# Value and query projections ahead of the key chain, and modulation sums tied in order, in a one-core transformer block

## The chip, the core and the metric

The kernel runs on one core of a Trainium2 chip. The time is that of the device from start to end of one execution, in microseconds (us). The engines are TensorE (PE, matrix products and transposes), VectorE (DVE), ScalarE (ACT), GpSimd (POOL) and SyncE (SP); here SP issues nearly all loads of weights, POOL most other transfers. Each engine runs its own list of instructions in order, and waits on semaphores for the others.

## What is computed

One layer of a diffusion transformer block for 256 latent and 256 context tokens of width 2048, in float32. In short:

```
mod = silu(c) @ w_ada + b_ada            # sh1, sc1, g1, sh2, sc2, g2
h = (x * (1 + sc1) + sh1) @ w_in         # all projections, context tokens for the states
branches = hyena(h), hgrn2(h), gated_deltanet(h)
y = sum(sigmoid(gate) * (branch @ w_branch)) @ w_out
x = layernorm(ALPHA * x + g1 * y) * ln1_g + ln1_b
x = layernorm(ALPHA * x + g2 * (relu(u @ w1) ** 2 @ w2)),  u = x * (1 + sc2) + sh2
```

The DeltaNet branch takes keys, values and queries through a convolution of three taps and a silu, and scales keys and queries to unit length in each head; it needs the products of keys with keys and of queries with keys in chunks of 64 (Gram blocks). The Hyena branch needs filters: a small network, a window and a transform (DFT) for each of 2 orders and 4 column blocks.

## The kernel before

**Weights.** A block of weights (128 x 1024 numbers, 512 KB) is loaded by SP into one of four slots with the tag `wraw` (L143), cast by ACT to a rounded high part `whi` (L138), and DVE takes the rest `wlo` (L139). PE then makes three products for each block (high x high, low x high, high x low; L218 to L220, L474, L476). There are four `whi` and three `wlo` slots. A slot is free again when its last reader is done; the loads wait for that on SP in their order.

**Order.** The program is written as one sequence, and a scheduler then decides the order on each engine, by its own model of durations; it may move an instruction ahead of others if the data allow it. `keep_in_program_order` ties an instruction behind the one of its engine that was written just before it. `beside(name, steps, rate)` puts a generator of small steps beside the stream of weights: each call of `wload` lets it advance by its rate.

**Modulation sums.** The columns of `w_ada` for g1, sh2, sc2 and g2 are not multiplied on PE: DVE sums them as `acc = acc + a * csil` (L531, the first by L529), for 8 parts of 16 units, 128 x 1024 each (`ada_parts`). A unit loads its tile `aw` into a `wraw` slot, one ahead. Parts 0 to 5 (96 units) run beside the projections from the start of `dn_early` on; parts 6 and 7 (32 units) are a part of `first_norm`, beside the feed-forward weights, and load into a ring of eight places, `awr`.

**DeltaNet.** `dn_early` takes the keys (`kch`, in PSUM tiles `psk`) through `conv_silu` (an ACT scaling, taps on DVE at L501 to L505 in the tile `cy`, silu on ACT), the gates (`dn_gates`), the unit lengths (`unit_rows`: transposes, squares and a root on ACT, a scaling on DVE at L570, transposes back) and the Grams; then the queries likewise; then four blocks of values, each followed by two filter steps.

**Filters.** A step of `filt` (`filters`) is: two loads on POOL, four products with the small network's output (L278), window (L279), skip (L283), sum and difference (L286, L287, `smdf`), a split into `shl` (ACT L138, DVE L139), 30 products with the transform (L234 to L236), copies out (L294).

**First layer norm.** The last block of `w_out` makes its two token tiles one after the other. For each: residual (L1396, L1400), statistics (`bn_stats` L1402, `bn_aggr` L1407), root on ACT and reciprocal (L1409, L1445), scaling of `xr` (L1450 on DVE, L1452 on ACT), transposes, modulation to `u2t` (L1460 on DVE, L1463 on ACT), split into `u` (L138, L139). The feed-forward products then begin.

Of the kernel before, what the change touches and what calls it, by code (L numbers as in the profile page):

```python
# [16 lines left out]
P = 128  # L17
# [63 lines left out]
def tile_block(ctx: ExitStack, tc: tile.TileContext, A: dict, out: bass.AP):  # L81
# [10 lines left out]
    def slot(shape, tag, name, dt=F32):  # L92
        uid[0] += 1
        return sbp.tile(shape, dt, name=f"{name}_{uid[0]}", tag=tag, bufs=NB[tag])
# [14 lines left out]
    def page(name, *shapes, dt=F32):  # L109

        return cut(slot([P, 2048], "k8", name, dt), shapes)
# [5 lines left out]
    def sc_ps():  # L117
        uid[0] += 1
        return psp.tile([P, 512], F32, name=f"ps_{uid[0]}", tag="ps", bufs=4)
# [50 lines left out]
    def transpose(dst_ps, src):  # L170
        nc.tensor.transpose(dst_ps, src, ident)
# [281 lines left out]
    def proj_cm(wap, col0, ah, al):  # L453

        ps = mm_ps()
        for kb in range(4):
            wh, wl = wload(wap, kb * 4, 4, col0, 256)
            for ch in range(2):
                for k in range(4):
                    kt = kb * 4 + k  # L460
                    cm_block(ps[:, ch * T:(ch + 1) * T], wh, wl, ch, k, ah[:, kt, :], al[:, kt, :],
                             kt == 0 and ch == 0, kt == KT - 1)
        return ps.rearrange("p (c t) -> p c t", c=2)
# [48 lines left out]

    acc_d = dram([8, P, W], "acc_d")

    def ada_parts(parts, ring=None):
        def load(b, kt):
            a = slot([P, W], "wraw", "aw") if ring is None else ring[:, (b * KT + kt) % 8]
            nc.sync.dma_start(out=a, in_=w_ada[kt * P:(kt + 1) * P, 2 * D + b * W:2 * D + (b + 1) * W])
            return a

        for b in parts:
            acc = slot([P, W], "k4", "acc")
            ahead = None
            for kt in range(KT):
                a = ahead if kt else load(b, kt)
                if kt < KT - 1:
                    ahead = load(b, kt + 1)
                if kt == 0:
                    ts_(out=acc, in0=a, scalar1=csil[:, 0, kt:kt + 1], scalar2=None, op0=MUL)  # L529
                else:  # L530
                    stt(out=acc, in0=a, scalar=csil[:, 0, kt:kt + 1], in1=acc, op0=MUL, op1=ADD)  # L531
                if kt == KT - 1:
                    dma(out=acc_d[b], in_=acc)
                yield

# [11 lines left out]
    def unit_rows(ch, tok, tiles, extra, nm):  # L549

        n = 4 * tiles
        ss = cst.tile([P, n], F32, name=f"ss_{nm}")
        for tl in range(tiles):
            pt = sc_ps()
            for j in range(4):
                transpose(pt[:, j * P:(j + 1) * P], ch[:, j, tl * P:(tl + 1) * P])
            copy(out=tok[:, tl, :], in_=pt)
            for j in range(4):
                junk = slot([P, P], "k1", "junk")
                act(out=junk, in_=tok[:, tl, j * P:(j + 1) * P], func=AF.Square,  # L560
                    accum_out=ss[:, 4 * tl + j:4 * tl + j + 1])
        act(out=ss, in_=ss, func=AF.Sqrt, bias=eps[:, 0:1])
        nc.vector.reciprocal(out=ss, in_=ss)
        if extra != 1.0:
            ts_(out=ss, in0=ss, scalar1=extra, scalar2=None, op0=MUL)
        for tl in range(tiles):
            pt = sc_ps()
            for j in range(4):
                t = tok[:, tl, j * P:(j + 1) * P]
                ts_(out=t, in0=t, scalar1=ss[:, 4 * tl + j:4 * tl + j + 1], scalar2=None, op0=MUL)  # L570
                transpose(pt[:, j * P:(j + 1) * P], t)
            copy(out=ch[:, :, tl * P:(tl + 1) * P], in_=pt.rearrange("p (j t) -> p j t", j=4))
# [84 lines left out]
    def dn_early():  # L657
        kch = page("kch", (4, 512))
        for r in range(4):
            conv_silu(psk[r], dck, r, True, kch[:, r, :])  # L660
        dn_gates()
        ktok = page("ktok", (4, 512))
        unit_rows(kch, ktok, 4, 1.0, "k")
        dma(out=kt_d.rearrange("t p c -> p t c"), in_=ktok)
        KKd, qch = page("kkq", (16, 64), (4, T))
        kxq, QKd = page("kxq", (24, 64), (8, 64))
        KX, QX = kxq[:, 0:16, :], kxq[:, 16:24, :]
        def grams(tl, rhs, diag, cross):
            ps = sc_ps()
            for j in range(4):  # L670
                sl = slice(tl * P, (tl + 1) * P)
                mm(ps[:, j * P:(j + 1) * P], kch[:, j, sl], rhs[:, j, sl], start=True, stop=True)
            pv = ps.rearrange("p (j f t) -> p j f t", j=4, f=2)
            for f in range(2):
                pr_ = slice(f * 64, (f + 1) * 64)
                copy(out=diag[pr_, tl * 4:(tl + 1) * 4, :], in_=pv[pr_, :, f, :])
                copy(out=cross[pr_, tl * 4:(tl + 1) * 4, :], in_=pv[pr_, :, 1 - f, :])

        for tl in range(4):
            grams(tl, kch, KKd, KX)  # L680
        for f in range(2):
            for rep in range(2):
                dma(out=dk[:, :, rep, f].rearrange("t q i j -> i (t q) j"), in_=KKd[f * 64:(f + 1) * 64])
        dma(out=kc_d, in_=kch)
        for blk in range(2):
            ps = proj_cm(w_in, C_DQ + blk * 256, uxh, uxl)
            for ch in range(2):
                r = 2 * blk + ch
                conv_silu(ps[:, ch, :], dcq, r, False, qch[:, r, :])
        unit_rows(qch, page("qtok", (2, 512), (2, 512))[0], 2, float(P) ** -0.5, "q")  # L690
        for tl in range(2):
            grams(tl, qch, QKd, QX)
        for f in range(2):
            for rep in range(2):
                dma(out=dq[:, :, rep, f].rearrange("t q i j -> i (t q) j"), in_=QKd[f * 64:(f + 1) * 64])
        dma(out=q_d, in_=qch)
        dma(out=kx_d, in_=kxq)

        for blk in range(4):
            pss = proj_cm_ctx(C_DV + blk * 256)  # L700
            for ch in range(2):
                r = 2 * blk + ch
                y = slot([P, 512], "k2", "vy")
                conv_silu(pss[ch], dcv, r, True, y)
                pt = sc_ps()
                for i in range(4):
                    transpose(pt[:, i * P:(i + 1) * P], y[:, i * P:(i + 1) * P])
                vt = slot([P, 4, P], "k2", "vt")
                copy(out=vt.rearrange("p a b -> p (a b)"), in_=pt)
                dma(out=v_d[:, :, r * P:(r + 1) * P].rearrange("t p c -> p t c"), in_=vt)  # L710
            next(filt)
            next(filt)

    def dn_systems():

# [76 lines left out]
            yield  # L792
        dma(out=dx[1], in_=M[64:P])

    beside("ada", ada_parts(range(6)), 1.0)
    dn_early()


# [762 lines left out]
```

## Time and profile before

| | before |
|---|---|
| median of 3 runs (range) | 2377.84 us (2377.05 to 2380.38) |
| profiled execution, its span | 2378.33 us, 2376.6 us |
| PE busy, mean granted clock | 96%, 0.982 |
| DVE, ACT, POOL busy | 69%, 45%, 8% |
| DMA queues, share of 16 engines | 69%, 215 GB/s |

The profile is one execution. PE is busy when a product is in its pipeline, which also counts products that run at half clock; so a stretch is read by both its idle time and its granted clock. A wait is put down to what ended it last.

### The profile page before, as it was taken

The page shows a single profiled execution, that of the slowest core. Times are in us where ns is not written, and L with a number is a line of the kernel's source. Part 1 is how long each engine was busy: PE and PEld are TensorE (multiplying, and loading weights), DVE is VectorE, ACT ScalarE, POOL GpSimd, SP SyncE. Part 2 cuts the span into 40 slices and gives each one's busy share as a digit, 9 for nine tenths or more (in the row PEclk, how much of TensorE's full clock was granted, in tenths as well). Part 3 has the DMA queues.
Part 4 walks back from the last instruction along what each step waited for, and adds up shares of the span by engine and source line. Part 5 has one row for each costly group of instructions (what it writes and reads, how often), then busy time and mean ns, then how long its engine had stood idle before and what let it go on. Part 6 is the DMA issues. An engine that isn't in the chain of part 4 may idle for free.

```text
span 2376.6 us, 32445 instructions
## 1 busy us (share of the span) xinstructions
PE 2280.7 (96%) x12353; PEld 1950.4 (82%) x12353; DVE 1649.0 (69%) x2183; ACT 1077.1 (45%) x1465; POOL 180.8 (8%) x297
## 2 busy tenths in 40 slices
PE   7999898999999999999999999996999999999998
PEld 4778688989989989777888878885888888888886
DVE  6777467877789898976566656658964655655667
ACT  6665444434433443534443444434544544543542
POOL 0000221000200000012030020000000000000000
PEclk9999999999999999999999999998999999999999
DMA  9958767778663333578786898677976666666664
GB/s 333 343 183 258 228 181 223 243 254 249 202 178 98 107 94 111 137 217 275 232 250 220 285 314 257 204 233 266 303 247 194 186 190 191 186 192 190 195 204 150
DMA packets 296072, 511.18 MB, mean 215 GB/s; under 512 B 17526, under 2 KB 155217, under 8 KB 293324
## 3 DMA queue, kind: packets, MB, share of 16 engines
q1 hardware_dynamic: 271488, 422.63, 56.2%
q0 software_dynamic: 21648, 82.01, 11.4%
q10 hardware_dynamic: 2780, 4.47, 0.6%
q8 instruction: 97, 1.59, 0.3%
q14 instruction: 59, 0.48, 0.1%
HBM read 474.59 MB, written 34.45 MB: 214 GB/s over the span
## 4 chain that ended last, share of the span: by engine, by line
PE 68%; DMA 7%; DVE 5%; issue 2%; ACT 1%; POOL 0%; DVEq 0%; SPq 0%; ACTq 0%; POOLq 0%
PE mm L474 10%; PE mm L490 8%; PE mm L491 8%; PE mm L489 8%; PE mm L476 5%; PE mm L220 3%; PE mm L218 3%; PE mm L219 3%; DMA aw<-in_w_ada_dram 3%; PE mm L815 3%; PE mm L816 3%; PE mm L814 3%; DVE wlo L139 2%; DMA wraw<-in_w_in_dram 2%; PE ps L1045 1%
## 5 line engine op out<-in xcount | busy, mean ns | idle before, releaser
L138 ACT CAST whi<-wraw 128x1024 fp32r<-128x1024 f32 x584 | 613.6, 1052 | 910.1 <-PE mm L491 253.9
L139 DVE TENSOR_TENSOR wlo<-wraw,whi 128x1024 fp32r<-128x1024 f32 x584 | 711.7, 1221 | 382.2 <-PE mm L490 148.1
L474 PE MATMUL mm<-u,whi 128*128 128x512 f32 x1024 | 361.8, 400 | 9.3 <-DVE u L139 7.6
L220 PE MATMUL mm<-uh,wlo 128*128 128x256 f32 (+1 forms) x1024 | 340.4, 336 | 3.4 <-DVE wlo L139 3.3
L218 PE MATMUL mm<-uh,whi 128*128 128x256 f32 (+1 forms) x960 | 317.9, 331 | 12.8 <-DVE cy L505 12.8
L219 PE MATMUL mm<-ul,whi 128*128 128x256 f32 (+1 forms) x960 | 318.4, 332 | 0.0
L476 PE MATMUL mm<-u,wlo 128*128 128x256 f32 x1024 | 283.9, 282 | 1.2 <-DVE wlo L139 1.1
L474 PEld LDWEIGHTS mm<-u,whi 128*128 128x128 f32 x1024 | 191.9, 189 | 55.2 <-DVE u L139 7.8
L220 PEld LDWEIGHTS mm<-uh,wlo 128*128 128x128 f32 x1024 | 198.4, 194 | 22.8 <-DVE wlo L139 4.2
L218 PEld LDWEIGHTS mm<-uh,whi 128*128 128x128 f32 x960 | 186.4, 194 | 29.8 <-issue 9.2
L219 PEld LDWEIGHTS mm<-ul,whi 128*128 128x128 f32 x960 | 186.2, 194 | 15.4 <-issue 0.7
L476 PEld LDWEIGHTS mm<-u,wlo 128*128 128x128 f32 x1024 | 194.7, 190 | 4.2 <-DVE wlo L139 1.9
L491 PE MATMUL mm<-whi,h 128*128 128x512 f32 x480 | 187.2, 390 | 0.0
L490 PE MATMUL mm<-wlo,h 128*128 128x512 f32 x480 | 186.9, 389 | 0.2 <-DVE wlo L139 0.2
L489 PE MATMUL mm<-whi,h 128*128 128x512 f32 x480 | 185.7, 391 | 0.0
L531 DVE SCALAR_TENSOR_TENSOR acc<-aw,csil,acc 128x1024 f32<-128x1024 f32 x90 | 115.2, 1280 | 95.4 <-DMA aw<-in_w_ada_dram 95.3
L815 PE MATMUL mm<-wlo,uh 128*128 128x512 f32 x384 | 153.1, 399 | 2.9 <-DVE wlo L139 2.9
L814 PE MATMUL mm<-whi,uh 128*128 128x512 f32 x384 | 150.2, 400 | 3.0 <-ACT fk L960 1.6
L816 PE MATMUL mm<-whi,ul 128*128 128x512 f32 x384 | 151.5, 395 | 0.0
L490 PEld LDWEIGHTS mm<-wlo,h 128*128 128x128 f32 x480 | 90.1, 188 | 19.6 <-DVE wlo L139 0.6
L489 PEld LDWEIGHTS mm<-whi,h 128*128 128x128 f32 x480 | 90.1, 188 | 19.4 <-issue 0.7
L491 PEld LDWEIGHTS mm<-whi,h 128*128 128x128 f32 x480 | 90.1, 188 | 18.9 <-issue 0.2
(517 smaller groups left out, 3992.2 us busy)
## 6 DMA issues: line engine op xcount, KB each, us to landing
wraw<-in_w_in_dram SPq DMA_DIRECT2D x264, 512.0 KB, 4.6
wraw<-in_w_ff_dram SPq DMA_DIRECT2D x256, 512.0 KB, 4.3
aw<-in_w_ada_dram SPq DMA_DIRECT2D x96, 512.0 KB, 4.6
raw<-in_w_ada_dram SPq DMA_DIRECT2D x32, 1024.0 KB, 5.7
wraw<-in_w_branch_dram SPq DMA_DIRECT2D x48, 512.0 KB, 5.0
wraw<-in_w_out_dram SPq DMA_DIRECT2D x32, 512.0 KB, 4.6
awr<-in_w_ada_dram SPq DMA_DIRECT2D x32, 512.0 KB, 8.5
g_d<-gate POOLq DMA_DIRECT2D x24, 256.0 KB, 5.0
```

What stands on the lines that cost most here:

```text
L138: copy(out=hi, in_=src)
L139: tt_(out=lo, in0=src, in1=hi.bitcast(F32), op=SUB)
L218: mm(ps, wh[:, k, cs], ah, start=first, stop=False, skip_group_check=True)
L219: mm(ps, wh[:, k, cs], al, start=False, stop=False, skip_group_check=True)
L220: mm(ps, wl[:, k, cs], ah, start=False, stop=last, skip_group_check=True)
L474: mm(pss[ch], wh[:, k, cs], a[:, kt].rearrange("p s t -> p (s t)"), start=(kt == 0), stop=False, skip_group_check=True)
L476: mm(pss[ch][:, 0:T], wl[:, k, cs], a[:, kt, 0], start=False, stop=(kt == KT - 1), skip_group_check=True)
L489: mm(pss[i], a, wh[:, k, :], start=(kt == 0), stop=False)
L490: mm(pss[i], a, wl[:, k, :], start=False, stop=False)
L491: mm(pss[i], b, wh[:, k, :], start=False, stop=(kt == nk - 1))
L815: mm(pg[i], a, wl[:, k, :], start=False, stop=False)
L816: mm(pg[i], c, wh[:, k, :], start=False, stop=(kt == KT - 1))
```

## The change

Three things change. `ada_parts` ties each sum to the DVE instruction written before it, for all 8 parts. The first 24 of the 96 units of parts 0 to 5 load into a ring of four places, `aring`, two units ahead; the other 72 use `wraw` slots as before, one ahead; the units of parts 6 and 7 load up to six ahead into their ring. In `dn_early`, values and queries are written in blocks between the steps of the key chain, and the filter steps between these.

```diff
     acc_d = dram([8, P, W], "acc_d")
 
-    def ada_parts(parts, ring=None):
...
+    in_turn = tc.keep_in_program_order
+
+    def ada_parts(parts, ring=None, places=8, first=None, pinned=False):
+
+        units = [(b, kt) for b in parts for kt in range(KT)]
+        first = len(units) if first is None else first
+        got = []
+
+        def load():
+            n = len(got)
+            b, kt = units[n]
+            a = ring[:, n % places] if n < first else slot([P, W], "wraw", "aw")
+            ld = nc.sync.dma_start(out=a, in_=w_ada[kt * P:(kt + 1) * P, 2 * D + b * W:2 * D + (b + 1) * W])
+            if pinned:
+                in_turn(ld)
+            got.append(a)
+
+        acc = None
+        for n, (b, kt) in enumerate(units):
+            ahead = places - 2 if n + 1 < first and not pinned else 1
+            while len(got) <= n or (len(got) < len(units) and len(got) <= n + ahead
+                                    and (len(got) < first or len(got) <= n + 1)):
+                load()
+            a = got[n]
+            if kt == 0:
+                acc = slot([P, W], "k4", "acc")
+                in_turn(ts_(out=acc, in0=a, scalar1=csil[:, 0, kt:kt + 1], scalar2=None, op0=MUL))
+            else:
+                in_turn(stt(out=acc, in0=a, scalar=csil[:, 0, kt:kt + 1], in1=acc, op0=MUL, op1=ADD))
+            if kt == KT - 1:
+                dma(out=acc_d[b], in_=acc)
+            yield
...
-        dn_gates()
-        ktok = page("ktok", (4, 512))
-        unit_rows(kch, ktok, 4, 1.0, "k")
-        dma(out=kt_d.rearrange("t p c -> p t c"), in_=ktok)
-        KKd, qch = page("kkq", (16, 64), (4, T))
-        kxq, QKd = page("kxq", (24, 64), (8, 64))
-        KX, QX = kxq[:, 0:16, :], kxq[:, 16:24, :]
-        def grams(tl, rhs, diag, cross):
...
-        for tl in range(4):
-            grams(tl, kch, KKd, KX)
...
-        for blk in range(2):
-            ps = proj_cm(w_in, C_DQ + blk * 256, uxh, uxl)
-            for ch in range(2):
-                r = 2 * blk + ch
-                conv_silu(ps[:, ch, :], dcq, r, False, qch[:, r, :])
...
-        for blk in range(4):
+        def values(blk):
...
-            next(filt)
-            next(filt)
...
+        values(0)
+        next(filt)
+        dn_gates()
+        KKd, qch = page("kkq", (16, 64), (4, T))
+        queries(0)
+        ktok = page("ktok", (4, 512))
+        unit_rows(kch, ktok, 4, 1.0, "k")
+        dma(out=kt_d.rearrange("t p c -> p t c"), in_=ktok)
+        queries(1)
+        next(filt)
+        kxq, QKd = page("kxq", (24, 64), (8, 64))
+        KX, QX = kxq[:, 0:16, :], kxq[:, 16:24, :]
+        values(1)
+        for tl in range(4):
+            grams(tl, kch, KKd, KX)
+        for f in range(2):
+            for rep in range(2):
+                dma(out=dk[:, :, rep, f].rearrange("t q i j -> i (t q) j"), in_=KKd[f * 64:(f + 1) * 64])
+        dma(out=kc_d, in_=kch)
+        next(filt)
+        next(filt)
+        values(2)
+        unit_rows(qch, page("qtok", (2, 512), (2, 512))[0], 2, float(P) ** -0.5, "q")
+        next(filt)
+        next(filt)
+        values(3)
+        for tl in range(2):
+            grams(tl, qch, QKd, QX)
+        for f in range(2):
+            for rep in range(2):
+                dma(out=dq[:, :, rep, f].rearrange("t q i j -> i (t q) j"), in_=QKd[f * 64:(f + 1) * 64])
+        dma(out=q_d, in_=qch)
+        dma(out=kx_d, in_=kxq)
+        next(filt)
+        next(filt)
...
-    beside("ada", ada_parts(range(6)), 1.0)
+    beside("ada", ada_parts(range(6), slot([P, 4, W], "m16", "aring"), 4, 24), 1.0)
     dn_early()
```

In the first layer norm the order on DVE was as follows, for the second token tile (`awr` are the ring's tiles, `st` the statistics, `mv_a` mean and variance):

```order
L139 TENSOR_TENSOR u_2288_13722<-u2t_13867,u_2288_13722 128x4x128
L529 TENSOR_SCALAR acc_14763<-awr_14762,csil 128x1024
L1402 BN_STATS st_13180<-xr_13178 128x6
L531 SCALAR_TENSOR_TENSOR acc_14763<-awr_14762,csil,acc_14763 128x1024
L1407 BN_AGGR mv_a_13927<-st_13180 128x2
L531 SCALAR_TENSOR_TENSOR acc_14763<-awr_14762,csil,acc_14763 128x1024
L1409 RECIPROCAL mv_a_13927<-mv_a_13927 128x1
L531 SCALAR_TENSOR_TENSOR acc_14763<-awr_14762,csil,acc_14763 128x1024
L1445 SCALAR_TENSOR_TENSOR mv_a_13927<-mv_a_13927 128x1
L1450 TENSOR_SCALAR xr_13178<-xr_13178,mv_a_13927 128x512 x2
L531 SCALAR_TENSOR_TENSOR acc_14763<-awr_14762,csil,acc_14763 128x1024
L1460 TENSOR_SCALAR u2t_13938<-ps_13933,gm,bm 128x128
```

And with the change (lines of the changed kernel are some 26 higher there):

```order
L139 TENSOR_TENSOR u_2265_13699<-u2t_13844,u_2265_13699 128x4x128
L1428 BN_STATS st_13157<-xr_13155 128x6
L1433 BN_AGGR mv_a_13904<-st_13157 128x2
L1435 RECIPROCAL mv_a_13904<-mv_a_13904 128x1
L1471 SCALAR_TENSOR_TENSOR mv_a_13904<-mv_a_13904 128x1
L1476 TENSOR_SCALAR xr_13155<-xr_13155,mv_a_13904 128x512 x2
L1486 TENSOR_SCALAR u2t_13915<-ps_13910,gm,bm 128x128
L1486 TENSOR_SCALAR u2t_13928<-ps_13923,gm,bm 128x128
L1486 TENSOR_SCALAR u2t_13915<-ps_13910,gm,bm 128x128
```

The first twelve rows hold five sums of the ring's tiles around the statistics and the scaling; with the change they stand over 60 rows further on, among the feed-forward blocks.

On DVE, beside one of the last filter steps, before:

```order
L279 TENSOR_TENSOR win_2956<-ps_2964,win_2956 128x512
L139 TENSOR_TENSOR wlo_3700<-wraw_3697,whi_3699 128x1024
L284 MEMSET win_2956 1x256
L283 TENSOR_TENSOR win_2956<-win_2956,sk_2968 1x256
L286 TENSOR_TENSOR smdf_2972<-win_2956 128x512
L287 TENSOR_TENSOR smdf_2972<-win_2956 128x512
L139 TENSOR_TENSOR wlo_3738<-wraw_3735,whi_3737 128x1024
L139 TENSOR_TENSOR shl_2975<-smdf_2972,shl_2975 128x1024
L139 TENSOR_TENSOR wlo_3771<-wraw_3768,whi_3770 128x1024
```

With the change, one filter step of the same kind, in a stretch that has no weight split between `wlo_3155`, 57 rows up, and `wlo_3188` (`hyc` is the Hyena convolution, `aring` and `aw` are tiles of w_ada in the ring and in weight slots):

```order
L543 SCALAR_TENSOR_TENSOR acc_2348<-aring_1237,csil,acc_2348 128x1024
L284 MEMSET win_2871 1x256
L502 SCALAR_TENSOR_TENSOR hyc_3137<-mm_3010,colB,hyc_3137 128x4x63
L543 SCALAR_TENSOR_TENSOR acc_2348<-aw_2782,csil,acc_2348 128x1024
L286 TENSOR_TENSOR smdf_2887<-win_2871 128x512
L287 TENSOR_TENSOR smdf_2887<-win_2871 128x512
L543 SCALAR_TENSOR_TENSOR acc_2348<-aw_3041,csil,acc_2348 128x1024
L139 TENSOR_TENSOR shl_2890<-smdf_2887,shl_2890 128x1024
L543 SCALAR_TENSOR_TENSOR acc_2348<-aw_3104,csil,acc_2348 128x1024
L139 TENSOR_TENSOR wlo_3188<-wraw_3185,whi_3187 128x1024
L139 TENSOR_TENSOR wlo_3218<-wraw_3215,whi_3217 128x1024
```

Before, weight splits alternate with the filter's rows; now the sums stand among them and the weights behind. On SP, the loads that lead to `wraw_3185` were these before, for the weights `wraw_3097` to `wraw_3238` of the same projections:

```order
L143 DMA wraw_3097<-in_w_in_dram 128x4x256
L518 DMA aw_3127<-in_w_ada_dram 128x1024
L143 DMA wraw_3130<-in_w_in_dram 128x4x256
L143 DMA wraw_3175<-in_w_in_dram 128x4x256
L518 DMA aw_3205<-in_w_ada_dram 128x1024
L143 DMA wraw_3208<-in_w_in_dram 128x4x256
L143 DMA wraw_3238<-in_w_in_dram 128x4x256
```

And with the change:

```order
L143 DMA wraw_3011<-in_w_in_dram 128x4x256
L527 DMA aw_3041<-in_w_ada_dram 128x1024
L527 DMA aring_1237<-in_w_ada_dram 128x1024 x4
L143 DMA wraw_3044<-in_w_in_dram 128x4x256
L143 DMA wraw_3074<-in_w_in_dram 128x4x256
L527 DMA aw_3104<-in_w_ada_dram 128x1024
L143 DMA wraw_3107<-in_w_in_dram 128x4x256
L143 DMA wraw_3152<-in_w_in_dram 128x4x256
L527 DMA aw_3182<-in_w_ada_dram 128x1024
L527 DMA aring_1237<-in_w_ada_dram 128x1024 x4
L143 DMA wraw_3185<-in_w_in_dram 128x4x256
```

The tiles in weight slots come as often as before, one for one or two weights; the ring's loads stand between them, and the sums that free the slots are now in the order of the program.

## Rows read from the trace of the kernel before

**Rows 1.** Work of each engine, PE's granted clock and DMA share in two stretches.
```profile
165.00:425.00 260.00, 238.80 (x1467) 211.56 (x1466) 167.00 (x267) 123.70 (x221) 48.17 (x75) 0.95 0.72 222
...
1600.00:1652.70 52.70, 34.68 (x163) 29.08 (x162) 40.53 (x69) 21.62 (x37) 2.70 (x4) 0.81 0.75 262
```

**Rows 2.** Waits of PE in 165 to 425: engine, line, releaser, us, times, longest.
```profile
PE mm L218 <- DVE cy L505: 12.8, 4, 6.0
```

**Rows 3.** Waits of DVE in the same stretch.
```profile
DVE acc L531 <- DMA aw<-in_w_ada_dram: 31.2, 15, 5.3
```

**Rows 4.** DVE's timeline ahead of the key convolutions: start, us, instruction [idle before].
```profile
160.37 1.28 DVE L531 SCALAR_TENSOR_TENSOR acc<-aw,csil,acc 128x1024 f32<-128x1024 f32 x1 [2.33 <-DMA aw<-in_w_ada_dram]
```

**Rows 5.** PE's timeline in the first layer norm.
```profile
1634.43 3.45 PE L171 MATMUL ps<-idon,xr 128*128 128x128 f32 x16 [10.41 <-DVE xr L1450]
1645.49 0.79 PE L474 MATMUL mm<-u,whi 128*128 128x512 f32 x1 [7.61 <-DVE u L139]
```

**Rows 6.** DVE's timeline in the first layer norm, both token tiles.
```profile
1615.02 0.26 DVE L1407 BATCH_NORM_AGGREGATE mv_a<-st 128x2 f32<-128x24 f32 x1
...
1615.92 1.00 DVE L1450 TENSOR_SCALAR xr<-xr,mv_a 128x512 f32<-128x512 f32 x2
...
1623.52 0.69 DVE L139 TENSOR_TENSOR u<-u2t,u 128x512 fp32r<-128x512 f32 x1
...
1628.59 0.75 DVE L529 TENSOR_SCALAR acc<-awr,csil 128x1024 f32<-128x1024 f32 x1
1629.25 0.69 DVE L1402 BATCH_NORM_STATS2 st<-xr 128x6 f32<-128x512 f32 x1
...
1633.75 1.00 DVE L1450 TENSOR_SCALAR xr<-xr,mv_a 128x512 f32<-128x512 f32 x2
1638.20 1.28 DVE L531 SCALAR_TENSOR_TENSOR acc<-awr,csil,acc 128x1024 f32<-128x1024 f32 x1 [3.46 <-DMA awr<-in_w_ada_dram]
...
1644.75 0.68 DVE L139 TENSOR_TENSOR u<-u2t,u 128x512 fp32r<-128x512 f32 x1
```

**Rows 7.** ACT's timeline in the first layer norm.
```profile
1620.24 2.73 ACT L1463 ACTIVATE u2t<-ps,bm,gm 128x128 f32<-128x128 f32 x7 [2.69 <-PE ps L171]
...
1635.56 0.46 ACT L1463 ACTIVATE u2t<-ps,bm,gm 128x128 f32<-128x128 f32 x1 [0.17 <-PE ps L171]
...
1639.84 0.81 ACT L1463 ACTIVATE u2t<-ps,bm,gm 128x128 f32<-128x128 f32 x2 [2.97 <-DVE u2t L1460]
```

**Rows 8.** DVE's sums of `awr`: ns min/median/max, first and last start.
```profile
L531 DVE SCALAR_TENSOR_TENSOR acc<-awr,csil,acc x30: 1231/1278/1285, 1629.8 to 1737.1; 128x1024 f32<-128x1024 f32 x30
```

**Rows 9.** Waits of PE in 1600 to 1740.
```profile
PE mm L474 <- ACT whi L138: 1.7, 1, 1.7
PE mm L476 <- DVE wlo L139: 1.1, 1, 1.1
```

**Rows 10.** DVE's groups in 165 to 425: busy us, mean ns, idle.
```profile
L139 DVE TENSOR_TENSOR wlo<-wraw,whi 128x1024 fp32r<-128x1024 f32 x44 | 53.4, 1214 | 22.9 <-PE mm L220 9.4 <-issue 5.7 <-ACT whi L138 4.4
L531 DVE SCALAR_TENSOR_TENSOR acc<-aw,csil,acc 128x1024 f32<-128x1024 f32 x32 | 41.0, 1281 | 31.2 <-DMA aw<-in_w_ada_dram 31.2
L279 DVE TENSOR_TENSOR win<-ps,win 128x512 f32<-128x512 f32 x16 | 11.0, 685 | 11.8 <-PE ps L278 11.8
...
L501 DVE SCALAR_TENSOR_TENSOR cy<-mm,colB,cy 128x252 f32<-128x252 f32 x8 | 3.8, 476 | 7.9 <-ACT cy L542 7.9
```

**Rows 11.** PE's timeline beside a filter step.
```profile
392.86 1.99 PE L278 MATMUL ps<-win,z 64*128 64x256 f32 x8
...
395.00 0.28 PE L218 MATMUL mm<-uh,whi 128*128 128x256 f32 x1
395.12 0.28 PE L219 MATMUL mm<-ul,whi 128*128 128x256 f32 x1
```

**Rows 12.** ACT's groups in 165 to 425.
```profile
L138 ACT CAST shl<-smdf 128x1024 fp32r<-128x1024 f32 x8 | 8.4, 1045 | 6.6 <-DVE smdf L287 6.6
```

**Rows 13.** DMA issues, whole run: KB each, median us to landing.
```profile
wraw<-in_w_in_dram SPq DMA_DIRECT2D x264, 512.0 KB, 4.6
```

More of the change, by code (lines that the diff above doesn't have):

```diff
@@ L513, in tile_block @@
     acc_d = dram([8, P, W], "acc_d")
-    def ada_parts(parts, ring=None):
[L516 to L534, printed above, removed]
+    in_turn = tc.keep_in_program_order
[26 more added lines that the diff above has]
+            yield
     def conv_silu(ps, w, r, with_ctx, out_t):
@@ L660, in dn_early @@
             conv_silu(psk[r], dck, r, True, kch[:, r, :])
-        dn_gates()
-        ktok = page("ktok", (4, 512))
-        unit_rows(kch, ktok, 4, 1.0, "k")
-        dma(out=kt_d.rearrange("t p c -> p t c"), in_=ktok)
-        KKd, qch = page("kkq", (16, 64), (4, T))
-        kxq, QKd = page("kxq", (24, 64), (8, 64))
-        KX, QX = kxq[:, 0:16, :], kxq[:, 16:24, :]
-        def grams(tl, rhs, diag, cross):
[L669 to L677, printed above, removed]
-        for tl in range(4):
-            grams(tl, kch, KKd, KX)
[L681 to L684, printed above, removed]
-        for blk in range(2):
-            ps = proj_cm(w_in, C_DQ + blk * 256, uxh, uxl)
-            for ch in range(2):
-                r = 2 * blk + ch
-                conv_silu(ps[:, ch, :], dcq, r, False, qch[:, r, :])
[L690 to L697, printed above, removed]
-        for blk in range(4):
+        def values(blk):
             pss = proj_cm_ctx(C_DV + blk * 256)
@@ L710, in dn_early, with queries, grams @@
                 dma(out=v_d[:, :, r * P:(r + 1) * P].rearrange("t p c -> p t c"), in_=vt)
-            next(filt)
-            next(filt)
+        def queries(blk):
+            ps = proj_cm(w_in, C_DQ + blk * 256, uxh, uxl)
+            for ch in range(2):
+                r = 2 * blk + ch
+                conv_silu(ps[:, ch, :], dcq, r, False, qch[:, r, :])
+        def grams(tl, rhs, diag, cross):
+            ps = sc_ps()
+            for j in range(4):
+                sl = slice(tl * P, (tl + 1) * P)
+                mm(ps[:, j * P:(j + 1) * P], kch[:, j, sl], rhs[:, j, sl], start=True, stop=True)
+            pv = ps.rearrange("p (j f t) -> p j f t", j=4, f=2)
+            for f in range(2):
+                pr_ = slice(f * 64, (f + 1) * 64)
+                copy(out=diag[pr_, tl * 4:(tl + 1) * 4, :], in_=pv[pr_, :, f, :])
+                copy(out=cross[pr_, tl * 4:(tl + 1) * 4, :], in_=pv[pr_, :, 1 - f, :])
+        values(0)
[26 more added lines that the diff above has]
+            grams(tl, qch, QKd, QX)
+        for f in range(2):
+            for rep in range(2):
[4 more added lines that the diff above has]
+        next(filt)
     def dn_systems():
```

## The prediction

> **What bounds the kernel now.** First the table of engine work by stretch, and there the clock and PE's idle time. PE is the busiest engine on the page, so only time in which PE waits or runs at a lower clock can be won. Two stretches lose visibly [rows 1]: 165 to 425 us (value, query and key work of the DeltaNet, with the Hyena filters beside it) and 1600 to 1652.7 us (the first layer norm).
>
> In the first, PE is busy for 238.8 of 260 us, so 21.2 us are idle, and the granted clock is 0.95, which is at most 0.05 x 260 = 13 us more. Of the idle time the largest entry is a projection that waits for the last tap of a convolution, since that tap frees its PSUM tile [rows 2]. DVE in turn waits there 31.2 us for loads of w_ada [rows 3]. The engine obeys its order: an accumulate whose load is late stands in front of taps that could run. At the start of the key chain one accumulate, ahead of the first tap, waits 2.33 us [rows 4].
>
> In the second, PE is busy for 34.7 of 52.7 us at clock 0.81. Two waits make it up: 10.41 us for the scaled second token tile, 7.61 us for the first split of `u` from it [rows 5]. In the DVE timeline the reason stands between: the first token tile goes from bn_aggr to the scaling in 0.90 us (1615.02 to 1615.92), the second has accumulates of `awr` between all its steps, from 1628.59 to 1633.75, and then an accumulate that waits 3.46 us for its load and holds the modulation (L1460) behind it [rows 6].
>
> The Trainium skill ("Perfetto Trace Analysis", section on the Tensor Engine instruction) calls the queues of ACT and DVE strict FIFO; the trace agrees, with the 3.46 us above.
>
> **The change, part by part.** The instructions are the same in kind, so PE's work at full clock does not change; only waits and the clock do.
>
> *1. Accumulates of `awr` leave the layer norm.* They are now tied behind the DVE instruction traced before them, and the order shows the norm without them. The accumulate at 1628.59 goes: bn_stats starts there instead of 0.66 later, bn_aggr 0.6 later, then 0.90 as in the first tile: scaling at about 1630.1 instead of 1633.75, 3.65 us earlier. The first ACT modulation of the second tile then moves from 1635.56 to 1631.9 [rows 7]. In the first tile, with no accumulate in the way, the first split of `u` was complete 1624.2 - 1620.24 = 3.96 us after the first such ACT instruction [rows 6, 7]; that gives 1635.9 instead of 1645.4. So PE's next projection starts **9.5 us** earlier. Bounds: if the alternation of ACT and DVE is as slow as before, only the 3.65 us remain; if the shorter waits spare PE the lower clock too, up to 13 (the clock of 0.81 costs at most 10 of 52.7 us, of which I give a third).
>
> *2. The same accumulates come later.* In before they end at 1737 [rows 8], and in 1600 to 1740 PE has two small waits for weights (1.7 and 1.1 us) that I put down to this density [rows 9]. Those go: -2.8. The 32 accumulates now lie between 1740 and the end, 1.28 us each, spread; price below: nothing, since DVE has room; above: the 2.8 us once more. I take 1.8, nearer the upper end, because a tied accumulate with a late load holds its queue. Net **-1.0**.
>
> *3. Key chain.* The four convolutions now stand ahead of the first accumulate, so the wait of [rows 4] goes from in front of them: some 2 us of PE's wait for that tap are won. Counted within part 4.
>
> *4. DeltaNet order, ring and ties.* By the order, each chain that PE waited for (gates, k lengths, k Grams) now has a projection of 24 to 48 matmuls beside it. This removes most of the 21.2 + 13 us, say all but 6 (the rest of the first wait, a half-clock stretch behind it, and one weight that loads late): 34 - 6 = 28 us won at most. But the same order has a hole. Between the split of `wlo_3155` and that of `wlo_3188` DVE has 57 rows and no weight: three filter steps and part of a fourth, three convolutions, the q rows and 11 accumulates. The reason stands on SP: four of the ten loads before `wraw_3185` are `aw` tiles in weight slots, and `wraw` has four slots. Each is freed by a tied accumulate, and these stand at the end of the hole. So no weight can load before the first of them.
>
> DVE's work in the hole, from [rows 10]: 11 accumulates at 1.28 and one first one at 0.75 are 14.0 with rounding; 4 filter splits like L139 at 1.21 are 4.8; 14 half-pages like L279 at 0.685 are 9.6; 16 taps at 0.47 are 7.5; the 18 short ones (row scalings, single rows, memsets) are 5 at 0.28 each, an estimate below the tap's 0.47. Together 41 us, of which the overlap of neighbours (1.28 shown, 1.20 from start to start) takes some 4: 37 us. PE has in the same stretch, by the order, 24 matmuls of the last block, 120 of the filters' transforms, 12 small L278, 36 transposes and Gram matmuls. At 0.12 from start to start for 256 columns, 0.24 for L278 (1.92 us for 8) [rows 11], and the 36 at 0.12 as an upper bound: 17.3 + 2.9 + 4.3 = 24.5 us. Serial parts (a filter step is L278, L279 to L287, ACT cast 1.05 [rows 12], DVE split 1.2, transform 3.6, and the next step's L278 stands behind it on PE) make the elapsed time longer: some 10 us of taps, accumulates and row scalings ahead of the first full step, three steps of 1.0 + 2.9 + 1.05 + 1.2 + 3.6 = 9.7, and 6 of accumulates between them, 45 us. After it the next weight needs its load, 4.6 us in the median [rows 13], much of it beside the last filter step. DVE enters the hole about one block (3 us) ahead of PE. So PE loses 45 - 24.5 - 3 = 17.5 us, bounds 9.5 (DVE work alone) and 24 (no lead, three more hops of about 1 us). To this comes the clock: PE idle in pieces, and in 165 to 425 the missing clock was up to 13 us on 21.2 idle, so up to 0.6 per us of wait; I take a third, 6, since 13 is an upper bound. Ahead of the hole the weights pass through one or two slots; a load and a cast (4.6 + 1.05) against 2.9 us of PE work per block: 3.5 once, since other PE work covers the second.
>
> Sum of part 4: -28 + 17.5 + 6 + 3.5 = **-1**. Bounds: -14 (hole 9.5, clock 3, single slots nothing) and +10 (hole 24, clock 10, 4 more).
>
> *5. 425 to 1600.* The remaining 72 ada units use weight slots with one ahead, as before; a tied one keeps its slot longer. Nothing, within 4 either way.
>
> Sum: -9.5 - 1.0 - 1 + 0 = **-11.5** on the profiled 2378.33 us, which is 0.5 us above the median of the runs: 2366.8, so **2367 us**.
>
> **The clock in the hole.** In [rows 1] a stretch with 18 us idle of 52.7 ran at 0.81. The Trainium skill ("TensorE: Matmul & The Clock Gate", section "HAM oscillation") describes a matmul engine that falls to half rate at every wait for data and pays for it anew each time. By that reading all PE work in the hole would run at half rate; of it the three transforms of 3.6 us stand on the chain, so 10.8 us in place of my 6, and the time would be 2372. The rows of 165 to 425, with 21.2 us idle and still a clock of 0.95, speak for the smaller price.
>
> **Rivals.** *A, the hole takes back the gain (no change or slower).* The four weight slots are held by tied accumulates, and while that lasts each new weight waits for load and cast, 5.65 us against 2.9 of PE work. For: SP's order. Against: past the hole each `aw` is accumulated within 2 to 4 blocks. With the upper bounds of part 4 (+10) the time is 2378; if single slots go on for 4 more blocks at 2.75 each, 2389. It turns from gain to loss when the early stage loses 11.5 us more than I sum, that is some 39 us in or near the hole.
>
> *B, the early stage keeps its gain.* PE's lead covers the hole, since filter transforms and value transposes fill it: -14 in place of -1, 2354. For: DVE alone needs 37 us, and PE has 24.5. Against: the serial steps.
>
> *C, the norm gains only the 3.65 us,* because L1460 and L1463 wait for each other whatever stands between: 2378.3 - 3.65 - 1 - 1 = 2373. For: in before ACT waited 2.97 us for DVE's L1460 at 1639.84 [rows 7]. Against: in the first tile the same pair ran through in 4 us.
>
> *D, the change does not do what it says:* tied accumulates take their waits along, and DVE's 31.2 us of waiting comes back in other places. The order speaks against it, as the ring is loaded two units ahead; 2376.
>
> **How the numbers follow.** My forecast with the norm's gain and an early stage near even: 0.48, own range 2361 to 2373. A 0.20 (two thirds of it within 0.2%, the rest beyond), B 0.18, C 0.09, D 0.05. About 0.2%, 4.8 us, is what a measurement of this kernel can tell from no change: faster means below 2373.1, slower above 2382.6. Faster: 0.46 of the forecast, all of B and half of C, 0.68. Slower: the rest of A and some unforeseen stall, 0.12. The same: 0.20. The range leaves out the far ends of A and B: **2353 to 2382**.
>
> **What would show it.** Right: in the norm no accumulate between bn_stats and the last split of `u`, the second PE wait below 3 us; a PE idle patch of 15 to 20 us during the last four filter steps, ended by a weight whose load began at an `aw` accumulate; DVE waits for `aw` before it nearly gone; no PE wait for `cy` above 3 us. Wrong: a lost patch above 35 us, new PE waits for `wlo` or `whi` in 425 to 1600 or 1740 to 2376, or a norm in which PE resumes at the old distance from its last `w_out` matmul (1623.6 to 1645.5).

## The result, and the profile after

| | before | after |
|---|---|---|
| median (range) | 2377.45 us (2372.8 to 2380.38) | 2433.38 us (2432.8 to 2434.57) |
| ratio, 95% interval | | 1.0238 (1.0225 to 1.0252) |
| profiled execution, span | 2378.33 us, 2376.6 us | 2434.57 us, 2432.9 us |

The kernel became 56 us slower. The page of the changed kernel shows as many instructions of PE as before and a smaller busy share; its mean granted clock was 0.973, where before had 0.982. First the row of before, then that of the change:

```profile
PE 2280.7 (96%) x12353; PEld 1950.4 (82%) x12353; DVE 1649.0 (69%) x2183; ACT 1077.1 (45%) x1465; POOL 180.8 (8%) x297
```

```profile
PE 2303.2 (95%) x12353; PEld 1961.3 (81%) x12353; DVE 1657.6 (68%) x2183; ACT 1079.0 (44%) x1467; POOL 177.2 (7%) x297
```

Since the work of PE is the same, the two traces can be laid beside each other at equal work: matmuls are counted from the start at what they take from start to start at full clock (227 ns for 512 columns, 120 for 256, 109 for 128), and the time is read at which each kernel has done so much. The difference to before then shows where time is lost and won. This table holds all kernels of this study, each by its profiled execution. The executions of one kernel lie up to 11 us apart (order_tail: 2365.79 to 2376.4 us, with the fastest one profiled), so differences of a few us between rows are not read:

| PE work done | 250 us | 350 | 650 | 900 | 1300 | 1450 | 1500 | 1600 | 2100 |
|---|---|---|---|---|---|---|---|---|---|
| before reaches it at | 312 | 427 | 738 | 990 | 1435 | 1588 | 1661 | 1766 | 2270 |
| after | -20.3 | +11.2 | +46.8 | +46.9 | +71.4 | +71.2 | +60.4 | +56.2 | +56.2 |
| untied_all | -13.4 | -11.1 | -5.0 | -5.0 | -7.0 | -7.0 | -9.6 | -9.2 | -9.2 |
| untied_slots | -19.7 | +6.1 | +13.3 | +13.3 | +13.7 | +13.7 | +1.7 | -2.4 | -2.4 |
| tie_only | +82.4 | +96.5 | +138.6 | +138.7 | +165.2 | +165.0 | +154.4 | +149.9 | +149.9 |
| tail_tie | +0.8 | -3.3 | +3.3 | +3.3 | -0.7 | -0.7 | -11.6 | -15.8 | -15.8 |
| no_slot | -21.9 | -24.2 | -23.6 | -23.5 | -34.4 | -34.4 | -44.9 | -49.0 | -49.0 |
| before_no_slot | +12.5 | +23.6 | +17.8 | +20.6 | +2.7 | +2.7 | -0.7 | -2.4 | -2.4 |
| old_order | -17.5 | +3.3 | +41.3 | +41.4 | +66.3 | +66.2 | +55.6 | +51.4 | +51.4 |
| new_order_tail | -12.4 | -10.3 | -4.7 | -4.7 | -7.3 | -7.3 | -19.5 | -24.0 | -24.0 |
| order_tail | -6.0 | +1.1 | +6.7 | +6.7 | +3.9 | +3.9 | -8.1 | -12.6 | -12.6 |
| part0_tied | -19.8 | -10.4 | -5.4 | -5.4 | -6.7 | -6.7 | -16.7 | -21.2 | -21.2 |

In the row "after", 20 us are won until before's 312 us, 31 are lost in the next 115 us, 36 more until 738, 24 between 990 and 1435, and 15 come back at the layer norm and behind it. Three stretches of equal work in which time is lost follow, each before and then now (busy time of PE is the second number, its clock stands behind POOL's numbers):

```profile
312.00:427.00 115.00, 107.22 (x749) 99.36 (x748) 79.91 (x114) 49.58 (x66) 25.34 (x41) 0.96 0.72 217
427.00:738.00 311.00, 303.79 (x1954) 277.16 (x1953) 249.78 (x308) 129.23 (x164) 26.90 (x39) 0.99 0.71 218
990.00:1435.00 445.00, 429.88 (x2201) 356.37 (x2201) 289.37 (x360) 201.34 (x285) 75.49 (x123) 0.98 0.81 254
```

```profile
291.70:438.20 146.50, 117.85 (x749) 106.70 (x748) 88.80 (x129) 58.08 (x103) 32.61 (x51) 0.85 0.61 189
438.20:784.80 346.60, 317.06 (x1969) 283.58 (x1968) 253.73 (x309) 129.62 (x161) 22.55 (x36) 0.96 0.66 200
1036.90:1506.40 469.50, 440.00 (x2201) 360.15 (x2200) 292.87 (x367) 200.69 (x284) 75.41 (x123) 0.96 0.79 242
```

PE's idle time grows by 20.9, 22.3 and 14.4 us in them. The rest of what is lost, 10.6, 13.3 and 10.1 us, is slower running at the lower granted clock: here each us of additional idle time cost 0.5 to 0.7 us more.

Ahead of them, from 165 to 292 us, the change did what it was made for. PE has one wait left there, where [rows 2] had 12.8 us for `cy`; and among DVE's waits from 165 to 425 none is of a sum for its load of w_ada, where [rows 3] had 31.2 us:

```profile
PE mm L218 <- DVE cy L505: 1.6, 1, 1.6
```

Then the hole comes. PE's waits from 292 to 430, and PE's busy time (second number) and clock (behind POOL's) in 300 to 430:

```profile
PE ps L234 <- ACT shl L138: 15.2, 4, 7.9
PE ps L171 <- DVE qtok L582: 6.7, 1, 6.7
```

```profile
300.00:430.00 130.00, 103.13 (x677) 94.64 (x675) 77.53 (x113) 50.64 (x90) 29.30 (x47) 0.83 0.60 188
```

The two waits shown are filter splits and query rows, the serial chain of the prediction; 27 us are idle, and the clock was 0.83. What holds the weights is read from SP. Its waits of weight loads for accumulates from 300 to 430, before and now (who waited, for whom, us in total, times, longest):

```profile
SPq L143 <- DVE acc L531: 4.5, 4, 1.4
```

```profile
SPq L143 <- DVE acc L543: 54.1, 5, 44.6
```

One wait for an accumulate (a sum of `ada_parts`) took 44.6 us. In SP's timeline it stands between the ring's loads and the next two weights:

```profile
317.33 0.34 SPq L527 DMA_DIRECT2D aw<-in_w_ada_dram  x1
325.80 4.29 SPq L527 DMA_DIRECT2D aring<-in_w_ada_dram  x4
374.82 2.78 SPq L143 DMA_DIRECT2D wraw<-in_w_in_dram  x2
```

And DVE's timeline has the split of a weight at 316.07, four sums of ring tiles from 325.16 on (the last three are shown), four more from 365.62 on, the first sum of a tile in a weight slot at 373.53, and 1.3 us behind its start, when it is done, the loads above are issued:

```profile
316.07 1.22 DVE L139 TENSOR_TENSOR wlo<-wraw,whi 128x1024 fp32r<-128x1024 f32 x1 [1.23 <-ACT whi L138]
...
325.81 3.93 DVE L543 SCALAR_TENSOR_TENSOR acc<-aring,csil,acc 128x1024 f32<-128x1024 f32 x3
...
352.00 0.27 DVE L299 MEMSET smdf<- 1x256 f32 x1 [5.84 <-ACT smdf L294]
...
365.62 1.15 DVE L543 SCALAR_TENSOR_TENSOR acc<-aring,csil,acc 128x1024 f32<-128x1024 f32 x1
```

```profile
373.53 1.26 DVE L543 SCALAR_TENSOR_TENSOR acc<-aw,csil,acc 128x1024 f32<-128x1024 f32 x1
...
381.88 1.23 DVE L139 TENSOR_TENSOR wlo<-wraw,whi 128x1024 fp32r<-128x1024 f32 x1 [2.36 <-ACT whi L138]
```

DVE itself waits in between, most of all 5.84 us at 352.00. The next weight split is at 381.88, 65.8 us after the last one. So the weight waited for a slot, the slot for its sum, and that sum for eight others tied in the order of the program behind convolutions and filter steps. The loads of `aw` before it were issued at 254.4, 272.1, 297.0 and 317.33 us, and none of their sums was done before 374.8: one slot after the other was lost to the weights, and from 317 on all four.

How long tiles of w_ada stay can be summed for the whole run, each from the issue of its load to the end of its sum. Half of them stayed for over 6.3 us before (the longest 12.7) and for over 20.9 now (120.3). The number of the four slots that they held, on average:

| us | 292 to 430 | 430 to 760 | 760 to 1000 | 1000 to 1500 |
|---|---|---|---|---|
| before | 0.53 | 0.58 | 0.09 | 0.37 |
| after | 3.08 | 2.03 | 1.22 | 1.46 |
| untied_slots | 2.75 | 0.61 | 0.09 | 0.35 |

The same thing in small goes on after 430 us. SP, DVE and ACT from 515 to 540, one timeline each:

```profile
515.10 0.37 SPq L143 DMA_DIRECT2D wraw<-in_w_in_dram  x1
516.24 0.34 SPq L527 DMA_DIRECT2D aw<-in_w_ada_dram  x1
521.23 0.37 SPq L143 DMA_DIRECT2D wraw<-in_w_in_dram  x1
527.29 0.34 SPq L527 DMA_DIRECT2D aw<-in_w_ada_dram  x1
531.12 1.69 SPq L143 DMA_DIRECT2D wraw<-in_w_in_dram  x2
```

```profile
526.04 1.22 DVE L139 TENSOR_TENSOR wlo<-wraw,whi 128x1024 fp32r<-128x1024 f32 x1 [3.87 <-ACT whi L138]
...
529.81 3.92 DVE L543 SCALAR_TENSOR_TENSOR acc<-aw,csil,acc 128x1024 f32<-128x1024 f32 x3
537.41 1.22 DVE L139 TENSOR_TENSOR wlo<-wraw,whi 128x1024 fp32r<-128x1024 f32 x1 [3.68 <-ACT whi L138]
```

```profile
524.96 1.05 ACT L138 CAST whi<-wraw 128x1024 fp32r<-128x1024 f32 x1 [5.01 <-DMA wraw<-in_w_in_dram]
...
536.34 1.04 ACT L138 CAST whi<-wraw 128x1024 fp32r<-128x1024 f32 x1 [7.17 <-DMA wraw<-in_w_in_dram]
```

Weights are issued singly, 6.1 us apart (515.10, 521.23), and then not for 9.9 us, until the first of three tied sums is made at 529.81, behind the split of a Hyena product (`btl`). The cast of the next weight waits 7.17 us for its load, and PE 7.2 us for that cast, the longest of these waits of PE (430 to 760; before had none for `whi` there, and 3.3 us for `wlo`):

```profile
PE mm L218 <- ACT whi L138: 11.2, 4, 7.2
PE mm L220 <- DVE wlo L139: 6.9, 6, 3.4
```

Behind that wait PE ran at a granted clock of 0.50, the lower of its two levels (1.2 GHz), for 5.4 us:

```profile
537.40:542.80 5.40, 4.91 (x21) 4.61 (x22) 3.64 (x3) 1.43 (x2) 0.00 (x0) 0.50 0.62 172
```

The layer norm is as forecast. DVE's and PE's timelines, for comparison with [rows 5, 6]:

```profile
1699.81 0.68 DVE L1428 BATCH_NORM_STATS2 st<-xr 128x6 f32<-128x512 f32 x1
1700.53 0.26 DVE L1433 BATCH_NORM_AGGREGATE mv_a<-st 128x2 f32<-128x24 f32 x1
...
1701.43 1.00 DVE L1476 TENSOR_SCALAR xr<-xr,mv_a 128x512 f32<-128x512 f32 x2
...
1706.35 0.69 DVE L139 TENSOR_TENSOR u<-u2t,u 128x512 fp32r<-128x512 f32 x1
```

```profile
1702.12 3.64 PE L171 MATMUL ps<-idon,xr 128*128 128x128 f32 x16 [6.83 <-DVE xr L1476]
1707.10 0.80 PE L474 MATMUL mm<-u,whi 128*128 128x512 f32 x1 [1.34 <-DVE u L139]
```

From bn_aggr to the scaling 0.90 us, as in the first tile; PE waits 6.83 and 1.34 us instead of 10.41 and 7.61. The sums of `awr` now run over 276 us, where [rows 8] had 107:

```profile
L543 DVE SCALAR_TENSOR_TENSOR acc<-awr,csil,acc x30: 1276/1278/1280, 1793.7 to 2069.7; 128x1024 f32<-128x1024 f32 x30
```

### The profile page after: what moved, and what is told of

It reads as the page before. It is cut to its first block, busy times and chain, and to the rows that moved or that the text cites. A ratio compares the mean times of both kernels' runs of the same rounds, so it can differ in the third digit from the quotient of the medians.

```text
span 2432.9 us, 32414 instructions
## 1 busy us (share of the span) xinstructions
PE 2303.2 (95%) x12353; PEld 1961.3 (81%) x12353; DVE 1657.6 (68%) x2183; ACT 1079.0 (44%) x1467; POOL 177.2 (7%) x297
## 4 chain that ended last, share of the span: by engine, by line
PE 69%; DMA 10%; issue 9%; DVE 7%; ACT 3%; POOL 1%; ACTq 0%; DVEq 0%; POOLq 0%; SPq 0%
PE mm L474 10%; PE mm L490 7%; PE mm L489 7%; PE mm L491 7%; DMA wraw<-in_w_in_dram 7%; PE mm L476 5%; PE mm L220 5%; PE mm L219 5%; PE mm L218 5%; DVE wlo L139 2%; PE mm L840 2%; PE mm L841 2%; PE mm L842 2%; ACT whi L138 1%; DMA raw<-in_w_ada_dram 1%
## 5 line engine op out<-in xcount | busy, mean ns | idle before, releaser
L218 PEld LDWEIGHTS mm<-uh,whi 128*128 128x128 f32 x960 | 185.4, 193 | 33.7 <-ACT whi L138 15.5
L489 PEld LDWEIGHTS mm<-whi,h 128*128 128x128 f32 x480 | 90.1, 188 | 19.5 <-issue 0.7
L139 DVE TENSOR_TENSOR wlo<-raw,ring 128x1024 fp32r<-128x1024 f32 x72 | 85.4, 1219 | 25.6 <-ACT ring L138 25.1
```

The lines of the kernel that those rows point to most:

```text
L139: tt_(out=lo, in0=src, in1=hi.bitcast(F32), op=SUB)
L218: mm(ps, wh[:, k, cs], ah, start=first, stop=False, skip_group_check=True)
L489: mm(pss[i], a, wh[:, k, :], start=(kt == 0), stop=False)
```

## The experiments

Theory 1: a tied sum keeps its tile of w_ada in a weight slot until the program's place for it comes; weights then have one slot or none, and PE starves. Theory 2: the new order of values and queries makes the hole by itself, by a chain of filter steps with too little work beside it.

**untied_all.** No ties at all:

```diff
-                in_turn(ts_(out=acc, in0=a, ...))
+                ts_(out=acc, in0=a, ...)
...
-                in_turn(stt(out=acc, in0=a, ...))
+                stt(out=acc, in0=a, ...)
```

> The change without any tie: new order of the projections and the ring of four places stay, all sums may float. Theory 1 (tied sums leave w_ada tiles in the weight slots, so weights can't load): the lost patch of 300 to 425 us and the losses after it go, but the sums return into the first layer norm: 2365 to 2385 us. Theory 2 (the new order of values and queries makes the hole by itself): the hole stays, 2420 us or more.

Measured: 2373.87 us, ratio 0.9982 (0.9967 to 0.9997). The hole is gone, with the new order in place; theory 2 is out as the cause of the loss. Of the 20 us won early, 13 are there without ties.

**untied_slots.** Ties only for units that load into a ring:

```diff
+            tie = in_turn if n < first else (lambda i: i)
...
-                in_turn(stt(out=acc, in0=a, ...))
+                tie(stt(out=acc, in0=a, ...))
```

> The change with ties only for units that load into a ring (the first 24 and awr); the 72 units in weight slots may float. Theory 1: the first hole stays, since units 24 and on follow the tied ring units in the same sum and so hold their slots as long (about 30 us lost between 300 and 430 us), but the later losses of the change (35 us between 430 and 760, 24 between 1060 and 1510) go: 2375 to 2390. If it is the ring's loads on SP and not the slots: the same as theory 1 here. Theory 2: no difference to the change, 2425 to 2440.

Measured: 2375.9 us, ratio 0.9982 (0.997 to 0.9993). The first loss stays (from -19.7 to +6.1), though no sum that reads a weight slot is tied: the first of them continue a sum whose units 16 to 23 are tied. (part0_tied, below, leaves these eight untied too, and loses 9 us there instead of 26.) The later losses fall from 60 to 8 us. SP's waits of weight loads for sums from 430 to 760 show it: in before, in the change, and here, where they are near before's again (L531, L543 and L544 are the same line of the three kernels):

```profile
SPq L143 <- DVE acc L531: 10.8, 7, 2.6
```

```profile
SPq L143 <- DVE acc L543: 28.9, 13, 5.5
```

```profile
SPq L143 <- DVE acc L544: 13.1, 9, 2.6
```

**tie_only.** The kernel before with every sum tied, old order, no ring for parts 0 to 5:

```diff
-    beside("ada", ada_parts(range(6)), 1.0)
+    beside("ada", ada_parts(range(6), first=0), 1.0)
```

(`ada_parts` as in the change.)

> The kernel before with ties on every sum, old order of projections, no ring for parts 0 to 5. Theory 1: all 96 units hold weight slots until their place in the program comes, so the stages up to 1500 us lose 30 to 80 us and the norm gains 15: 2390 to 2440. Theory 2: only the norm's gain, about 2362.

Measured: 2531.12 us, ratio 1.064 (1.0617 to 1.0663): ties alone, with 96 instead of 72 units in weight slots, lose 165 us up to the norm, more than twice what I expected. A weight load waited for a sum 57 times:

```profile
SPq L143 <- DVE acc L543: 158.6, 57, 36.0
```

**tail_tie.** The kernel before, ties for parts 6 and 7 alone, with up to six of their loads ahead, as in the change:

```diff
+            tie = in_turn if n < first else (lambda i: i)
...
+    beside("ada", ada_parts(range(6), first=0), 1.0)
```

> The kernel before, with ties (and up to six loads ahead) for the sums of parts 6 and 7 alone. Both theories: the norm and the feed-forward start gain what they gained in the change (71.2 - 56.2 = 15 us), nothing else moves: 2360 to 2365. Rival: the gain hung on something else of the change, such as a later arrival at the norm; then 2370 to 2378.

Measured: 2359.6 us, ratio 0.992 (0.99 to 0.9939). The norm gives 10.9 us (from -0.7 to -11.6) and the start of the feed-forward 4.2 more, with no other part of the change. The six loads ahead without ties are in untied_all, which won 2.2 us in the same stretches (from -7.0 to -9.2); so most of the gain goes with the ties. PE's wait for `cy` (165 to 430) is as before:

```profile
PE mm L218 <- DVE cy L505: 14.1, 4, 5.9
```

**no_slot.** The change with all ties, but units 24 to 95 load nothing, so the kernel leaves out g1, sh2 and a part of sc2:

```diff
         def load():
             n = len(got)
             b, kt = units[n]
+            if n >= first:
+                got.append(None)
+                return
...
+            if a is None:
+                a = acc
+            if kt == 0 and n >= first:
+                in_turn(nc.vector.memset(acc, 0.0))
```

> The change with all its ties, but units 24 to 95 load no tile of w_ada and take up no weight slot: their sums read the sum itself (the part's first unit clears it), so 36 MB of loads and the true values of g1, sh2 and part of sc2 are left out. Ties, order on DVE and number of sums stay. Theory 1 (what costs is that tied sums hold weight slots): the lost patch at 300 to 430 us and the later losses go, the gain before 292 us and that of the norm stay, 2325 to 2350. Rival (the ties cost by themselves, since a tied sum stands in DVE's order ahead of splits): 2400 to 2435.

Measured: 2330.04 us, ratio 0.979 (0.9769 to 0.9812). The ties stand where they stood, the slots are free, and 103 us of the change's time are gone. So the ties do not cost this by their place in DVE's order, nor by the ring's loads in SP's, which are still there. In 300 to 430 PE is busy for 124.2 us at clock 0.97, against 103.1 at 0.83, and the queues moved more, 209 GB/s against 188, so what the queues can carry did not hold PE up in the change:

```profile
300.00:430.00 130.00, 124.16 (x911) 116.55 (x910) 102.84 (x143) 67.60 (x110) 29.35 (x47) 0.97 0.68 209
```

**before_no_slot.** The same loads left out of the kernel before:

```diff
         def load(b, kt):
+            if ring is None and b * KT + kt >= 24:
+                return None
```

(and the sums as in no_slot.)

> The kernel before (no ties, old order), but units 24 to 95 load no tile of w_ada and take up no weight slot; their sums read the sum itself, so the same loads and values are left out as in the change's variant without slots (2330 us, against 2433). If most of that variant's 103 us came from fewer loads and not from the slots, this one gains as much against before: 2300 or less. Theory 1: without ties the tiles leave their slots early anyway, so only DVE's waits for loads (62 of 95 us, mostly beside idle time) and little PE time are won: 2345 to 2365.

Measured: 2375.91 us, ratio 0.9982 (0.9972 to 0.9992). I had expected 2345 to 2365. The run does not single out the price of the loads, since the sums moved as well: with no load to wait for, 74 of them start between 250 and 500 us, where before has 25, and PE's waits for the cast of a filter's split grow from 6.1 to 17.8 us (165 to 430). Its early stage lost 24 us to before at equal work, and the time from 427 us on won them back. So how the 103 us of no_slot divide between slots and loads stays open. That the slots cost is shown by untied_slots, with all loads in place: as soon as the tiles leave early, the later losses go.

**old_order.** The change with the old `dn_early`:

```diff
-        values(0)
-        next(filt)
         dn_gates()
...
```

> The change with the old order of the DeltaNet projections; ties and ring stay. Theory 1: the hole is there too, since units 24 and on again follow 24 tied ones: 2410 to 2450. Theory 2 (the new order makes the hole): 2362, the norm's gain alone.

Measured: 2429.7 us, ratio 1.0212 (1.0186 to 1.0237). The loss is there without the new order, and so is most of the early gain (-17.5). SP's longest wait for a sum, 300 to 430:

```profile
SPq L143 <- DVE acc L543: 43.8, 5, 37.1
```

**new_order_tail.** New order and ring, ties for parts 6 and 7 alone:

```diff
+            tie = in_turn if places == 8 else (lambda i: i)
```

> New order, ring of four for the first 24 units, ties only for the sums of parts 6 and 7. Theory 1: the 10 us that the change without ties had won by 500 us and the norm's 11 to 15 add up: 2353 to 2358. Rival: the two gains overlap, 2362.

Measured: 2358.0 us, ratio 0.9905 (0.9883 to 0.9927).

**order_tail.** The same without the ring (tail_tie with the new `dn_early`):

```diff
+        values(0)
+        next(filt)
         dn_gates()
...
```

> New order without the ring (all 96 units in weight slots, untied), ties only for parts 6 and 7. If the early gain came from the order of the projections: 2353 to 2358, as with the ring. If it came from the ring's four places: about 2362, as with the tail alone.

Measured: 2371.56 us, ratio 0.9969 (0.9956 to 0.9981), slower than both expectations. The new order without the ring wins 6 us at most and has lost them by 427 us; with the ring (new_order_tail) 10 us are left there, and the median is 13.6 us lower. So the early gain needs the ring. Whether that is because its tiles take no weight slot, or because they load further ahead, was not separated. Against tail_tie, which differs by the order alone, this run is 12 us slower: without the ring the new order loses time.

**part0_tied.** New order and ring, ties for the 16 units of part 0 and for parts 6 and 7:

```diff
+            tie = in_turn if places == 8 or n < KT else (lambda i: i)
```

> New order and ring; ties only for the 16 units of part 0, all of which load into the ring, and for parts 6 and 7. Theory 1: ties are harmless where no weight slot hangs on them, so the gain of the change before 292 us (20 us; 13 without ties) is kept and the hole does not open, with the norm's 11 to 15: 2345 to 2355. Rival: the 20 us were an advance that any version pays back at the filters, since the same work has only been moved: 2355 to 2360, as with ties on the tail alone.

Measured: 2358.37 us, ratio 0.9915 (0.9896 to 0.9934). The rival's 2355 to 2360 came, not the 2345 to 2355 of theory 1. The early 20 us are there, and half of them is paid back at the filters, as the rival said: PE waits (165 to 430) for the cast of a filter step's split, while the sums of tiles in weight slots are free to move:

```profile
PE ps L234 <- ACT shl L138: 11.3, 2, 7.1
```

Three versions with ties on the tail, tail_tie, new_order_tail and part0_tied, are 0.8 to 0.95% faster than the kernel before; their intervals overlap, so which of them is the best stays open.

## Why the prediction was wrong

The sum had five terms, -11.5 us in all; the profiled executions differ by +56.2, 68 more. By the table:

- *1, the norm, -9.5:* right. The time from the end of `w_out` to the first feed-forward matmul fell from 21.9 (1623.6 to 1645.5) to 12.3 us (1694.8 to 1707.1), by 9.6; the table has 10.8 us between 1450 and 1500 us of work, and tail_tie 10.9. The steps were as forecast too: 0.90 us from bn_aggr to the scaling, no sum in between.
- *2, the later sums of `awr`, -1.0:* right in kind, too small; 4.2 us were won behind the norm (tail_tie: 4.2), where PE's idle time of 3.0 us (1661 to 1766 before) is gone. The price of 1.8 for the spread sums was not there: from 1600 us of work on the difference does not move.
- *3 and 4, DeltaNet stage, -1:* wrong in size by 12. The gain before the hole was 20.3 where 28 was the sum, which had counted all waits to 425 us; the part ahead of the hole was won almost whole (from 165 us on PE was idle for 13.4 us before, to 312, and for 1.6 now, to 292). The hole and what follows cost 31.5 by 427 us where 27 was. The place and the reason were as told: a stretch between `wlo_3155` and `wlo_3188` ended by the sum of an `aw` tile, filter chains within it. Its added idle time of PE came out as summed, 20.9 us where 17.5 and 3.5 stood. The term that was too small is the clock: 10.6 us where 6 stood. The prediction's other reading of the clock had 10.8, but that is luck in the number: it slowed the three transforms of the chain as a whole, while of the 110 transform matmuls from 316 to 382 us about half ran slowly, which cost 5 us, and the rest lies elsewhere. On DVE the hole took 65.8 us where I had 45. DVE was busy for 39.6 of them, near the 37 of the sum, and waited for the rest, 9.0 us of it for ACT's copies of filter products (5.84 us at 352.00 before L299), which the sum left out.
- *5, 425 to 1600, nothing within 4:* here the prediction failed. 36 us were lost between 427 and 738 us, 24 between 990 and 1435, 60 of the 68. The step said "a tied one keeps its slot longer" and priced that at nothing, without working it out; rival A gave the reason, that each `aw` is accumulated within 2 to 4 blocks of its load. But a tile then stays for some 21 us in place of 6, and with one or two of four slots taken for so long (2.0 and 1.5 on average, where before had 0.6 and 0.4) the weights at times go through the rest one by one, and each then costs a load, a cast and a split. untied_slots shows it: 60 us become 8 when these sums are untied and the tiles leave early. Rival A had the mechanism and gave it "4 more blocks at 2.75 each"; the runs had it in both stretches. Between 738 and 990 us nothing was lost, with 1.2 slots taken; PE was never idle there, in either kernel.

Part 4 had already said why: no weight can load before the tied sum. It was used for the one place where the order shows a hole, and not for the rest, where the order shows none: 57 rows without a weight are seen in a list, a queue of loads that is short of slots is not. Nor do the waits of weight loads for weight splits show it. They were 156.8 us from 430 to 760 before and 139.6 with the change: loads wait for a free slot whenever they run ahead of PE. What can be asked of a new order is how long each tile will hold its slot. The Trainium skill ("Perfetto Trace Analysis", section "Optimization Strategy") says that a gap which repeats on the engine that should be saturated can mean too few buffers for the next tile; the trace agrees, with PE's waits of 11.2 us for `whi` and 6.9 for `wlo` from 430 to 760, shown above.

In the working of part 4 two numbers do not follow, and neither changes the outcome: the lower bound is -15.5 with the terms given, not -14, and the rows of SP show three `aw` loads among the ten before `wraw_3185`; the fourth tile, `aw_2782`, was loaded earlier.

That untied sums in slots still make the first loss (untied_slots) was in the prediction only in that the freeing sums "stand at the end of the hole"; the runs show that a tie also holds back the later units of the same sum.

## What to carry to other kernels

A tie that fixes an instruction's place on its engine also fixes when its input's buffer comes free: before tying, ask which pool the input sits in and who else loads into it. Sums whose tiles all had a buffer of their own could be tied at a gain here (the norm and behind it, 15 us). Tying the tiles that share the weights' slots cost 57 us (the change against untied_slots), and tying ring tiles whose sum goes on in such slots cost some 16 (untied_slots against part0_tied, up to 427 us). Idle time is not the whole price: each us of it cost 0.5 to 0.7 us more here through the clock. And two changes with opposite signs should be read at equal work of the bounding engine, which separated +71 and -15 here in one table.

## What was unexpected of the hardware

A load of 512 KB that was issued alone took 3.7 us until the cast of it began (521.23 to 524.96), though the queues were busy for only 0.51 of that time. With a cast and a split behind it, a weight that goes through one free slot takes 6.1 us from issue to issue (515.10 to 521.23), more than twice the 2.9 us that PE needs for its 24 matmuls at 0.12. And PE's losses went on when the weight was there: after the 7.2 us of waiting it ran at the lower clock level for 5.4 us.
